# Scales of a modulation moved to TensorE, copies of rows moved to DMA queues, and low parts of the retention moved from GpSimd to VectorE

## The chip, the cores and the metric

The kernel runs on one core of a Trainium2 chip. The metric is the device time of one execution in microseconds (us); lower is better. PE is TensorE, DVE is VectorE, ACT is ScalarE, POOL is GpSimd, SP is the engine whose queue issues most DMAs (SPq in the views).

## The reference, cut to what matters

Two layers (`DEPTH = 2`) of a block with three token mixers run over 512 image tokens `x` and 256 context tokens `z`, with 1024 features. Before each mixer the tokens are scaled and shifted per feature; scale and shift come from a conditioning vector:

```
mod_x = jax.nn.silu(c) @ p['w_ada'] + p['b_ada']          # 6 x 1024 values, for x
mod_z = jax.nn.silu(c_ctx) @ p['w_ada'] + p['b_ada']      # and for z
sh1x, sc1x, g1x, sh2x, sc2x, g2x = split(mod_x, 6)
hx = x * (1.0 + sc1x) + sh1x
hz = z * (1.0 + sc1z) + sh1z
mix_x, mix_z = token_mixers(hx, hz, ...)   # hx @ w_in, then retention, neighborhood attention, MLA
x = layer_norm(ALPHA * x + g1x * mix_x)
x = layer_norm(ALPHA * x + g2x * sq_relu_mlp(x * (1.0 + sc2x) + sh2x))
```

The retention scores each chunk against itself with a decay mask in two directions, adds the product of the queries with a running state, normalises per head and gates the result. Its queries and keys are rotated first (`x1*cos - x2*sin`, `x1*sin + x2*cos`). The second layer leaves out the outputs of `z`.

## The kernel before, in words

Feature-major tiles of 128 features by 512 (or 256) tokens stay on the chip. A float32 product is done as three products in a rounded float32 form (`mm3`, L428 to L430): each operand is split into a high part, rounded by ACT (`hi_of`, L381), and a low part, the rest, by a subtraction (`lo_of`, L384) that runs on DVE unless another engine is handed in. Weights come from DRAM in units of 128 x 1024 (512 KB) through SP's queue (`fetch_in`, L390) and are split the same way.

The order on each engine is set by a scheduler that works out due times for the whole program; within it generators of work (`fill`, `pend`) are fed between the steps of the attention pipelines, so that TensorE has projections to do while the chains of an attention item run on the other engines. Every queue, SP's and POOL's among them, runs its instructions in the order that the scheduler gave it.

**The opening** (`opening`, `inputs`, L1575 to L1615). For each k of 8 feature tiles two units of `w_ada` are loaded (kind 1 is the scale, kind 0 the shift), then the tile of `x` and of `z`. `modulation` makes scale and shift from a unit by a product with the conditioning vector, summed along the row: an instruction of DVE at L496 (128 x 1024, named CUSTOM_DVE_ANT_0 in the trace). Three of the four sums of a tile are DVE's; the fourth (the shift for `z`) is a product by POOL (L492) and a sum by ACT (L493). `affine_split` then writes the scaled tile twice by ACT (L581 in full, L584 rounded) and the low part by POOL (L384, names `op<-mh,op`). TensorE multiplies the tile with four units of `w_in` (`outer`; 12 products of 512 columns and 9 of 256 per tile).

**The copies of rows.** `stacked` puts the high part of a head on 64 partitions and copies it, and the low part, to the other 64 (L665, L666, by POOL); the keys of the neighborhood attention (names `nop`, `nlo`) and the queries of the retention (`op`) go through it. L1311 does the same for the states of the retention (`st`).

**The retention** (`Retention`). `prep` makes the operands for two heads: the rotation multiplies by cosine on DVE (L1220) and by sine on POOL (L1221, `rb`) after four DMAs that swap rows (L1219, `rb<-ra`); the decayed keys are split with the low part on POOL (`t<-ktf,t`); the decay tables are multiplied by a mask on POOL (L1269). `item` has three steps: s0 scores, decay (L1349) and a split of the result with the low part on POOL (`pf<-pf,pf`), s1 products and statistics (L1373 to L1391, with a power on POOL at L1386), s2 the transposed output (L1398).

Of the kernel before, what the change touches and what calls it, by code (L numbers as in the profile page):

```python
# [16 lines left out]
DEPTH = 2  # L17
# [36 lines left out]

# [40 lines left out]
def pack_weights(inp):  # L98
# [10 lines left out]
    for l in range(DEPTH):  # L109
# [5 lines left out]
        for c in range(48):  # L115
            put(("ada", c), wa[:, 128 * c : 128 * c + 128].T)
        for n, c in (("rq", 2), ("rk", 2), ("nq", 4), ("nk", 4), ("pq", 2), ("pkv", 2), ("g0", 8), ("g1", 8), ("g2", 8)):
# [193 lines left out]
def block_kernel(ctx, tc, xT, zT, cond, wu, sp, bias, tab, out):  # L311
# [82 lines left out]


    spt = []
    for l in range(DEPTH):
# [54 lines left out]

    MOD_ADJUST = ((0, 1), (1, 1), (0, 0.5 / ALPHA), (0, 1), (1, 1), (0, 1.0 / ALPHA))

# [6 lines left out]
    def conditioning(banks):  # L461

        v = sgl("silu")
        v, h = v[:, :16], v[:, 16:32]
        fetch_in(v, cond)
        act.activation(h, v, AF.Tanh, scale=0.5)
        dve.scalar_tensor_tensor(v, h, 1.0, v, ALU.add, ALU.mult)
        cs = cond_tiles()
        for t in range(2):
            for i in range(2):  # L470
                ps = banks()
                spread(ps, 0, v[:, 8 * t + 4 * i : 8 * t + 4 * i + 4], 512)
                dst = cs[t][:, 512 * i : 512 * i + 512]
                if i:
                    dve.tensor_copy(dst, ps)
                else:
                    act.activation(dst, ps, AF.Copy)
        return cs

# [5 lines left out]

    def modulation(l, c, raw, cs, pinned=False, shared=()):

        for t in shared:  # L490
            h = dbl("prod")
            pool.tensor_tensor(h, raw, cs[t], op=ALU.mult)  # L492
            act.activation(h, h, AF.Copy, scale=0.5, accum_out=mods[l][:, c, t : t + 1])  # L493
            dve.tensor_scalar(mods[l][:, c, t : t + 1], mods[l][:, c, t : t + 1], spt[l][:, SP_BADA + c : SP_BADA + c + 1], 0.0, op0=ALU.add, op1=ALU.add)
        for t in [t for t in range(2) if t not in shared and (t == 0 or c < 16 or l < DEPTH - 1)]:
            i = dve.tensor_tensor_reduce(cs[2], raw, cs[t], 0.5, spt[l][:, SP_BADA + c : SP_BADA + c + 1], ALU.mult, ALU.add, mods[l][:, c, t : t + 1])  # L496
            if pinned:
                tc.keep_in_program_order(i)
        m = mods[l][:, c, : 2 if c < 16 or l < DEPTH - 1 else 1]
        add, mul = MOD_ADJUST[c // 8]  # L500
        if (add, mul) != (0, 1):
            dve.tensor_scalar(m, m, float(add), float(mul), op0=ALU.add, op1=ALU.mult)

# [149 lines left out]
    def stacked(dst, src, scale, view, mixed):  # L653

        xs, lows = dst
        for o, x in enumerate(xs):
            r, q = (slice(0, 64), slice(64, 128))[:: 1 - 2 * o]  # L660
            hi_of(view(x)[r], src[r], scale)
            lo = x[q] if mixed else lows[o][r]
            dve.scalar_tensor_tensor(R(view(lo)), src[r], scale, view(x)[r], ALU.mult, ALU.subtract)
            if not mixed:
                pool.tensor_copy(R(x[q]), x[r])  # L665
                pool.tensor_copy(R(lows[o][q]), lows[o][r])  # L666

# [483 lines left out]
    class Retention:  # L1151
# [39 lines left out]
        def prep(self, p2):  # L1191
# [20 lines left out]
            def rotated(name, scale, zneed, mixed):  # L1212
# [7 lines left out]
                dve.tensor_tensor(a, a, cos, op=ALU.mult)  # L1220
                pool.tensor_tensor(b, b, sin, op=ALU.mult)  # L1221
                dve.tensor_tensor(a, a, b, op=ALU.add)
# [26 lines left out]
            for src, i0 in ((k32, 0), (kz32, 4)):  # L1249
# [4 lines left out]
                for i in range(nt):  # L1254
# [5 lines left out]
                    hi_of(t[:, :256], f)  # L1260
                    lo_of(t[:, 256:], f, t[:, :256], pool)
                yield cost(512)

            gm = new_tiles(512, 2)
            for o in range(2):
                for dr in range(2):
                    c = 4 * dr + 2 * p2 + o
                    act.activation(gm[o][:, 256 * dr : 256 * dr + 256], dist[:, 256 * dr : 256 * dr + 256], AF.Exp, scale=lg[:, c : c + 1])
                pool.tensor_tensor(gm[o], gm[o], mask, op=ALU.mult)  # L1269

# [33 lines left out]
            for which in range(2):  # L1304
                for dr in range(2):
# [4 lines left out]
                    lo_of(v[own, :, 1], src, v[own, :, 0])  # L1310
                    pool.tensor_copy(R(t[other]), t[own])  # L1311

# [15 lines left out]
        def item(self, p2, o, c):  # L1328
# [4 lines left out]
            def s0():  # L1333
# [11 lines left out]
                for d, parts in ((0, ((0, 0, 256), (384, 0, 128))), (384, ((256, 256, 256), (0, 384, 128)))):  # L1345
                    f = sgl("pf")[:, :384]
                    e = 0
                    for a, b, n in parts:
                        dve.tensor_tensor(f[:, e : e + n], sc[:, a : a + n], gm[o][:, b : b + n], op=ALU.mult)  # L1349
                        e += n  # L1350
                    split_into((t[:, d : d + 384], u[:, d : d + 384]), f, pool)
                st["p"] = [(t[:, :384], u[:, :384]), (t[:, 384:], u[:, 384:])]
# [218 lines left out]
    def opening():  # L1571
# [11 lines left out]
        hx, hz = new_operand(NX, KT), new_operand(NZ, KT)  # L1583
        cs = conditioning(bank_t)
        busy(N_IDLE[1], cs[1])
        bx = [bank_d(), bank_d(), bank_t(), bank_t()]
        bz = [bank_s()[:, :256], bank_s()[:, :256], bank_d()[:, :256]]

        def inputs(k):

            for kind in (1, 0):
                raw = dbl("ada")
                fetch_in(raw, wu[IDX[0, "ada", 8 * kind + k]])
                modulation(0, 8 * kind + k, raw, cs, shared=(1,) if kind == 0 else ())
            t, u = sgl("x0"), sgl("z0")[:, :NZ]
            fetch_in(t, xT[128 * k : 128 * k + 128, :])
            fetch_in(u, zT[128 * k : 128 * k + 128, :])
            return t, u

        ws = first_weights(0, (0, 1), spare=True)  # L1600
        tiles = inputs(0)
        ws += first_weights(0, (2, 3), spare=True)
        for k in range(KT):
            ahead = inputs(k + 1) if k + 1 < KT else None
            for h, t, tok in ((hx[k], tiles[0], 0), (hz[k], tiles[1], 1)):
                affine_split(h, t, mod(0, 1, k, tok), mod(0, 0, k, tok), pool, True)
            tiles = ahead
# [257 lines left out]
```

## Time and profile before

| what | us |
|---|---|
| median of 3 runs (2626.32 to 2634.21) | 2628.12 |
| profiled execution, its own time | 2628.3 |
| its span, first to last instruction | 2626.5 |
| PE busy, share of the span | 2515.5 (96%) |
| DVE busy | 1782.5 (68%) |
| ACT busy | 1155.7 (44%) |
| POOL busy | 333.4 (13%) |
| mean granted clock of PE, share of full | 0.980 |

The span is cut in the views in stretches of time. A row of such a table gives the busy time of each engine in the stretch, the clock that TensorE was granted (1.00 is 2.4 GHz, 0.50 is 1.2 GHz, values between them a mix of the two levels) and what the DMA engines moved. In a row on waits the engine on the left stood idle until the one on the right was done.

### The profile page before, as it was taken

To read this page: it belongs to the slowest core of one execution; us is meant where nothing else is said; L and a number is where in the kernel's file an instruction comes from. 1 tells how busy PE (TensorE), PEld (TensorE's weight loads), DVE (VectorE), ACT (ScalarE), POOL (GpSimd) and SP (SyncE) were. 2 spreads that over 40 slices of the span, in tenths; PEclk is the share of its full clock that TensorE was granted. 3 is DMA by queue.
4 is the path that set the end of the run, shared out by engine and by line. 5 is a ranking of instruction groups with operands and counts; after the bars stand their busy time and mean duration, and the time that the engine had idled before them with its cause. 6 is when DMAs were issued, how large, how long until landed. Compare 5 with 4: busy or idle time off the path is not lost. (4 is left out here: it accounts for less than half of the span.)

```text
span 2626.5 us, 39849 instructions
## 1 busy us (share of the span) xinstructions
PE 2515.5 (96%) x15218; PEld 2234.2 (85%) x15218; DVE 1782.5 (68%) x3434; ACT 1155.7 (44%) x2176; POOL 333.4 (13%) x321
## 2 busy tenths in 40 slices
PE   6999999998999998999999999999999899999997
PEld 4899998987888877888888878889888788988887
DVE  8566556777878886667556767665668768744457
ACT  4555545564333345322222446554555434732325
POOL 6201102234202000000000000010214310000000
PEclk7999999999999999999999999999999999999998
DMA  6222223423565633444444424323343356433333
GB/s 241 80 82 81 70 81 110 128 79 112 200 229 169 200 120 103 125 131 137 125 132 137 136 83 138 98 82 105 109 145 99 113 192 193 137 105 96 97 97 121
DMA packets 142995, 329.43 MB, mean 125 GB/s; under 512 B 16978, under 2 KB 54738, under 8 KB 142804
## 3 DMA queue, kind: packets, MB, share of 16 engines
q1 hardware_dynamic: 132436, 311.15, 38.6%
q10 hardware_dynamic: 10368, 15.73, 1.6%
q8 instruction: 120, 1.97, 0.3%
q14 instruction: 71, 0.58, 0.1%
HBM read 288.27 MB, written 36.45 MB: 124 GB/s over the span
## 5 line engine op out<-in xcount | busy, mean ns | idle before, releaser
L428 PE MATMUL pd<-op,wsp 128*128 128x512 f32 (+1 forms) x3080 | 1074.0, 350 | 29.1 <-ACT op L584 9.6
L429 PE MATMUL pd<-op,wsp 128*128 128x512 f32 (+1 forms) x3080 | 1071.9, 348 | 6.5 <-POOL op L384 4.9
L430 PE MATMUL pd<-op,wsp 128*128 128x512 f32 (+1 forms) x3080 | 1065.3, 347 | 11.6 <-DVE wsp L384 11.6
L428 PEld LDWEIGHTS pd<-op,wsp 128*128 128x128 f32 x3080 | 588.4, 191 | 104.7 <-ACT op L584 11.5
L430 PEld LDWEIGHTS pd<-op,wsp 128*128 128x128 f32 x3080 | 588.2, 191 | 83.9 <-DVE wsp L384 13.9
L429 PEld LDWEIGHTS pd<-op,wsp 128*128 128x128 f32 x3080 | 589.9, 192 | 78.0 <-POOL op L384 8.5
L381 ACT ACTIVATE wsp<-wraw 128x1024 fp32r<-128x1024 f32 x319 | 336.4, 1055 | 425.5 <-PE pd L430 295.0
L384 DVE TENSOR_TENSOR wsp<-wraw,wsp 128x1024 fp32r<-128x1024 f32 x319 | 392.0, 1232 | 190.6 <-ACT wsp L381 189.8
L643 PE MATMUL pd<-wsp,op 128*128 128x256 f32 x704 | 201.8, 287 | 2.1 <-DVE pr L753 1.6
L645 PE MATMUL pd<-wsp,op 128*128 128x256 f32 x704 | 200.5, 285 | 0.9 <-DVE wsp L384 0.9
L644 PE MATMUL pd<-wsp,op 128*128 128x256 f32 x704 | 200.2, 285 | 0.0
L1752 DVE TENSOR_TENSOR rl<-rl 128x256 f32<-128x256 f32 (+1 forms) x104 | 58.9, 567 | 149.8 <-ACT rl L1751 149.8
L384 DVE TENSOR_TENSOR pt<-pst,pt 128x512 fp32r<-128x512 f32 (+1 forms) x208 | 121.7, 604 | 47.1 <-ACT pt L381 45.3
L1522 POOL TENSOR_TENSOR tiny<-tiny,half 128x2 f32<-128x2 f32 (+1 forms) x8 | 9.0, 1128 | 1129.1 <-DVE tiny L1521 621.9
L1751 ACT ACTIVATE rl<-pd 128x256 f32<-128x256 f32 (+1 forms) x104 | 51.7, 498 | 226.3 <-PE pd L430 226.1
L1766 DVE TENSOR_TENSOR t<-pd,t 128x512 f32<-128x512 f32 (+1 forms) x132 | 80.9, 616 | 88.3 <-PE pd L430 87.9
L643 PEld LDWEIGHTS pd<-wsp,op 128*128 128x128 f32 x704 | 136.0, 193 | 3.2 <-issue 2.4
L645 PEld LDWEIGHTS pd<-wsp,op 128*128 128x128 f32 x704 | 135.8, 193 | 1.4 <-DVE wsp L384 1.4
L644 PEld LDWEIGHTS pd<-wsp,op 128*128 128x128 f32 x704 | 135.9, 193 | 0.1
L381 ACT ACTIVATE pt<-pst 128x512 fp32r<-128x512 f32 (+1 forms) x208 | 105.1, 529 | 51.7 <-PE pst L595 39.4
L612 PE MATMUL pso<-pt,t 128*128 128x256 f32 x704 | 114.7, 292 | 7.8 <-DVE ntx L619 2.4
L496 DVE CUSTOM_DVE_ANT_0 cond<-graw,cond,sp 128x1024 bf16<-128x1024 f32 x80 | 102.4, 1280 | 18.8 <-DMA graw<-wu 18.6
(280 smaller groups left out, 3667.4 us busy)
## 6 DMA issues: line engine op xcount, KB each, us to landing
wraw<-wu SPq DMA_DIRECT2D x327, 512.0 KB, 3.7
graw<-wu SPq DMA_DIRECT2D x56, 512.0 KB, 3.7
ada<-wu SPq DMA_DIRECT2D x40, 512.0 KB, 5.5
gg<-gate ACTq DMA_DIRECT2D x48, 256.0 KB, 2.0
gl<-gg SPq DMA_DIRECT2D x48, 256.0 KB, 3.3
zbias<-bias SPq DMA_DIRECT2D x64, 128.0 KB, 2.3
t<-vd SPq DMA_DIRECT2D x28, 256.0 KB, 5.3
gd<-gt SPq DMA_DIRECT2D x40, 128.0 KB, 2.2
```

What stands on the lines that cost most here:

```text
L381: act.activation(R(dst), src, AF.Copy, scale=scale)
L384: (eng or dve).tensor_tensor(R(dst), src, hi, op=ALU.subtract)
L428: pe.matmul(ps, R(a[0]), R(b[0]), start=start, stop=False)
L429: pe.matmul(ps, R(a[0]), R(b[1]), start=False, stop=False)
L430: pe.matmul(ps, R(a[1]), R(b[0]), start=False, stop=stop)
L496: i = dve.tensor_tensor_reduce(cs[2], raw, cs[t], 0.5, spt[l][:, SP_BADA + c : SP_BADA + c + 1], ALU.mult, ALU.add, mods[l][:, c, t : t + 1])
L612: pe.matmul(o, R(vts[k]), R(pts[k]), start=k == 0, stop=k == n - 1)
L643: pe.matmul(ps, R(a[0]), R(w[0][:, o : o + 256]), start=k == 0, stop=False)
L644: pe.matmul(ps, R(a[1]), R(w[0][:, o : o + 256]), start=False, stop=False)
L645: pe.matmul(ps, R(a[0]), R(w[1][:, o : o + 256]), start=False, stop=k == nk - 1)
L1752: dve.tensor_tensor(t, t, t, op=ALU.mult)
L1766: dve.tensor_tensor(a, ps, a, op=ALU.add)
```

## The change

Five edits. (1) In the opening the scale (kind 1) is computed on TensorE: a float32 product of the unit, now packed with features of the input on the partitions, with the two conditioning vectors (8 products of 2 columns per tile), and one DVE instruction that reads the result; DVE computes both sums of the shift; POOL's product and ACT's sum are gone. `+1` is folded into the bias once, so the small instructions at L502 go for the scales. (2) `affine_split` in the opening uses DVE for the full tile and for the low part. (3) The first tile's inputs are loaded ahead of the first weights, and the conditioning vector ahead of everything. (4) The copies of rows in `stacked` and of the states are DMAs on SP's queue. (5) The retention's low parts (`t<-ktf`, `pf`) and the sine product are DVE's, and the mask is applied to two of the four 128-column blocks of a table.

```
+ADA_PE = [(0, c) for c in range(8, 16)]
...
-            put(("ada", c), wa[:, 128 * c : 128 * c + 128].T)
+            w = wa[:, 128 * c : 128 * c + 128]
+            put(("ada", c), fm(w) if (l, c) in ADA_PE else w.T)
...
+    def modulation_pe(ps, l, c, raw, v):
+        for k in range(KT):
+            pe.matmul(ps, raw[:, 128 * k : 128 * k + 128], v[:, :, k], start=k == 0, stop=k == KT - 1)
+        m = mods[l][:, c, :]
+        dve.tensor_scalar(m, ps, 0.5, spt[l][:, SP_BADA + c : SP_BADA + c + 1], op0=ALU.mult, op1=ALU.add)
+        adjust(m, c)
...
-        for t in shared:
-            h = dbl("prod")
-            pool.tensor_tensor(h, raw, cs[t], op=ALU.mult)
-            act.activation(h, h, AF.Copy, scale=0.5, accum_out=mods[l][:, c, t : t + 1])
...
-                pool.tensor_copy(R(x[q]), x[r])
-                pool.tensor_copy(R(lows[o][q]), lows[o][r])
+                sync.dma_start(x[q], x[r])
+                sync.dma_start(lows[o][q], lows[o][r])
...
-                pool.tensor_tensor(b, b, sin, op=ALU.mult)
+                dve.tensor_tensor(b, b, sin, op=ALU.mult)
...
-                    lo_of(t[:, 256:], f, t[:, :256], pool)
+                    lo_of(t[:, 256:], f, t[:, :256])
...
-                pool.tensor_tensor(gm[o], gm[o], mask, op=ALU.mult)
+                ends, cut_off = (t.rearrange("p (e n) -> p e n", n=128)[:, 0:4:3] for t in (gm[o], mask))
+                pool.tensor_tensor(ends, ends, cut_off, op=ALU.mult)
...
-                    pool.tensor_copy(R(t[other]), t[own])
+                    sync.dma_start(t[other], t[own])
...
-                    split_into((t[:, d : d + 384], u[:, d : d + 384]), f, pool)
+                    split_into((t[:, d : d + 384], u[:, d : d + 384]), f)
...
-                modulation(0, 8 * kind + k, raw, cs, shared=(1,) if kind == 0 else ())
+                if kind:
+                    modulation_pe(bank_o()[:, :2], 0, 8 * kind + k, raw, v)
+                else:
+                    modulation(0, k, raw, cs)
...
-                affine_split(h, t, mod(0, 1, k, tok), mod(0, 0, k, tok), pool, True)
+                affine_split(h, t, mod(0, 1, k, tok), mod(0, 0, k, tok), dve)
```

What follows are places in the order of the instructions. First DVE in the opening, in the kernel before, for one tile and the start of the next; ada_214 is the unit of a scale, ada_219 of a shift, and the rows without an input read out a sum.

```order
L496 ISA cond_138,mod_103<-ada_214,cond_138,sp_93 128x1024
L496 ISA mod_103 128x1
L496 ISA cond_138,mod_103<-ada_214,cond_139,sp_93 128x1024
L496 ISA mod_103 128x1
L502 TENSOR_SCALAR mod_103<-mod_103 128x2
L496 ISA cond_138,mod_103<-ada_219,cond_138,sp_93 128x1024
L496 ISA mod_103 128x1
L494 TENSOR_SCALAR mod_103<-mod_103,sp_93 128x1
```

The same place in the changed kernel: pso_300 is the bank into which TensorE wrote the scale of the tile after the next, x_55 and z_56 are the tiles to be split, ada_310 is the unit of a shift.

```order
L494 TENSOR_SCALAR mod_105<-pso_300,sp_95 128x2
L596 TENSOR_SCALAR mh_318<-x_55_265,mod_105 128x512
L596 TENSOR_SCALAR mh_322<-z_56_266,mod_105 128x256
L389 TENSOR_TENSOR op_128<-mh_318,op_128 128x512
L512 ISA cond_141,mod_105<-ada_310,cond_141,sp_95 128x1024
L512 ISA mod_105 128x1
L389 TENSOR_TENSOR op_135<-mh_322,op_135 128x256
L512 ISA cond_141,mod_105<-ada_310,cond_142,sp_95 128x1024
L512 ISA mod_105 128x1
```

Two of the four large sums remain on DVE, and the two tiles and their low parts come to it. TensorE in the opening, in the kernel before, at the end of one tile and the start of the next (op_123 and op_130 are the tiles of `x` and `z`, op_124 the next of `x`):

```order
L429 MATMUL pss_174<-op_130,wsp_183 128x256
L430 MATMUL pss_174<-op_130,wsp_183 128x256
L429 MATMUL pd_175<-op_130,w_204 128x256
L430 MATMUL pd_175<-op_130,w_205 128x256
L428 MATMUL pd_169<-op_124,wsp_178 128x512
L428 MATMUL pd_170<-op_124,wsp_183 128x512
```

The same place in the changed kernel (op_134 is the tile of `z`, op_128 the next of `x`, ada_298 the unit of a scale):

```order
L436 MATMUL pss_177<-op_134,wsp_206 128x256
L437 MATMUL pss_177<-op_134,wsp_206 128x256
L436 MATMUL pd_178<-op_134,w_211 128x256
L492 MATMUL pso_300<-v_cond,ada_298 128x2 x8
L437 MATMUL pd_178<-op_134,w_212 128x256
L435 MATMUL pd_172<-op_128,wsp_201 128x512
L435 MATMUL pd_173<-op_128,wsp_206 128x512
```

The eight products of a scale stand one place ahead of the end of a tile. POOL in the first pass of the retention of layer 0, in the kernel before (t_727x are low parts of decayed keys, op copies of queries, pf low parts of an item):

```order
L384 TENSOR_TENSOR t_7274<-ktf_7299,t_7274 128x256
L384 TENSOR_TENSOR t_7274<-ktf_7303,t_7274 128x256
L1269 TENSOR_TENSOR t_7307<-t_7307,dist_6996 128x512 x2
L665 CAST op_7394<-op_7394 64x256 x2
L666 CAST op_7395<-op_7395 64x256
L1221 TENSOR_TENSOR rb_7373<-rb_7373,rot_6993 128x512
L666 CAST op_7395<-op_7395 64x256
L665 CAST op_7382<-op_7382 64x512 x2
L666 CAST op_7383<-op_7383 64x512
L384 TENSOR_TENSOR pf_7415<-pf_7416,pf_7414 128x384
L666 CAST op_7383<-op_7383 64x512
L384 TENSOR_TENSOR pf_7415<-pf_7421,pf_7414 128x384
```

POOL at the same place in the changed kernel, in full (rs are powers of the statistics, nyz a sum of the attention before):

```order
L640 TENSOR_TENSOR nyz_6720<-tz_6966,fo_6970 64x256
L1401 TENSOR_TENSOR rs_7160<-rs_7160,half 128x4
L1401 TENSOR_TENSOR rs_7290<-rs_7290,half 128x4
L1284 TENSOR_TENSOR t_7342<-t_7342,dist_7031 128x2x128 x2
L1401 TENSOR_TENSOR rs_7482<-rs_7482,half 128x4
```

Of the twelve rows one pair is left, half as wide. SP's queue in the neighborhood attention of layer 0, in the kernel before (zbias is the bias of one item, wraw a weight):

```order
L888 DMA my_3_256_850<-my_4215 128x256
L1035 DMA zbias_4029<-bias 128x256 x3
L390 DMA wraw_5403<-wu 128x1024
L1035 DMA zbias_4029<-bias 128x256 x2
L390 DMA wraw_5706<-wu 128x1024
```

The same place in the changed kernel:

```order
L901 DMA my_3_256_885<-my_4250 128x256
L1048 DMA zbias_4064<-bias 128x256 x2
L678 DMA nop_4695<-nop_4695 64x512
L679 DMA nlo_4696<-nlo_4696 64x512
L678 DMA nop_4695<-nop_4695 64x512
L679 DMA nlo_4696<-nlo_4696 64x512
L678 DMA nop_4705<-nop_4705 64x256
L679 DMA nlo_4706<-nlo_4706 64x256
L678 DMA nop_4705<-nop_4705 64x256
L1048 DMA zbias_4064<-bias 128x256
L395 DMA wraw_5438<-wu 128x1024
L679 DMA nlo_4706<-nlo_4706 64x256
```

Eight copies of a pair of heads now stand between the loads of biases and weights.

## Rows read from the trace of the kernel before

**Rows 1.** Page, part 1: busy us of TensorE and GpSimd, instructions.

```profile
PE 2515.5 (96%) x15218; PEld 2234.2 (85%) x15218; DVE 1782.5 (68%) x3434; ACT 1155.7 (44%) x2176; POOL 333.4 (13%) x321
```

**Rows 2.** Stretches of 50 us: length, busy us per engine, granted clock, DMA, GB/s.

```profile
0.00:50.00 50.00, 33.51 (x100) 22.43 (x101) 43.05 (x51) 22.20 (x35) 28.98 (x18) 0.79 0.81 286
50.00:100.00 50.00, 42.93 (x254) 36.53 (x254) 36.82 (x63) 29.85 (x56) 24.71 (x15) 0.90 0.23 75
...
650.00:700.00 50.00, 39.09 (x241) 35.28 (x240) 40.41 (x115) 18.67 (x39) 20.23 (x22) 0.93 0.34 115
...
800.00:850.00 50.00, 48.76 (x308) 43.68 (x307) 44.41 (x128) 16.82 (x33) 15.33 (x12) 1.00 0.58 174
...
2000.00:2050.00 50.00, 44.43 (x289) 40.49 (x288) 38.78 (x88) 23.73 (x53) 24.56 (x24) 0.90 0.37 105
```

**Rows 3.** Waits of TensorE in 0 to 100 us: total, times, longest.

```profile
PE pd L428 <- ACT op L584: 8.6, 5, 4.1
PE pd L429 <- POOL op L384: 4.9, 6, 2.5
PE pss L428 <- ACT op L584: 4.8, 3, 2.5
```

**Rows 4.** Timeline of the opening, VectorE: start, duration, what.

```profile
40.71 3.50 DVE L496 CUSTOM_DVE_ANT_0 cond<-ada,cond,sp 128x1024 bf16<-128x1024 f32 x1
...
44.14 0.20 DVE L494 TENSOR_SCALAR mod<-mod,sp 128x1 f32<-128x1 f32 x1
44.27 1.27 DVE L496 CUSTOM_DVE_ANT_0 cond<-ada,cond,sp 128x1024 bf16<-128x1024 f32 x1
...
59.39 1.27 DVE L496 CUSTOM_DVE_ANT_0 cond<-ada,cond,sp 128x1024 bf16<-128x1024 f32 x1
```

**Rows 5.** The same timeline, GpSimd.

```profile
40.73 2.40 POOL L492 TENSOR_TENSOR prod<-ada,cond 128x1024 f32<-128x1024 f32 x1
```

**Rows 6.** Timeline of TensorE: products at the lower and higher clock, sums in float32.

```profile
25.66 0.63 PE L429 MATMUL pst<-op,w 128*128 128x512 f32 x1
...
26.08 0.63 PE L430 MATMUL pst<-op,w 128*128 128x512 f32 x1
...
55.99 0.39 PE L429 MATMUL pst<-op,w 128*128 128x512 f32 x1
56.22 0.39 PE L430 MATMUL pst<-op,w 128*128 128x512 f32 x1
...
78.94 1.84 PE L720 MATMUL pso<-ones,sq 128*128 128x1 f32 x16
```

**Rows 7.** VectorE, 500 to 710 us, by shape: busy us, mean ns, idle before.

```profile
L606 DVE TENSOR_SCALAR p<-p,tiny 128x512 f32<-128x512 f32 x16 | 8.8, 549 | 0.3
...
L384 DVE TENSOR_TENSOR t<-pd,t 128x256 fp32r<-128x256 f32 x14 | 5.8, 414 | 0.3 <-ACT t L381 0.2
...
L1222 DVE TENSOR_TENSOR ra<-ra,rb 128x512 f32<-128x512 f32 x4 | 2.8, 688 | 2.8 <-POOL rb L1221 2.7
```

**Rows 8.** Stretches of 5 us in the opening, columns as in Rows 2.

```profile
10.00:15.00 5.00, 5.00 (x13) 2.30 (x11) 4.78 (x5) 0.34 (x1) 3.26 (x1) 1.00 1.05 401
```

**Rows 9.** Waits of TensorE in 500 to 720 us.

```profile
PE pst L1373 <- DVE ro L1377: 6.5, 1, 6.5
...
PE pd L1253 <- DVE ra L1222: 2.3, 1, 2.3
```

**Rows 10.** Timeline of GpSimd inside the wait of 6.5 us.

```profile
646.26 2.72 POOL L1269 TENSOR_TENSOR t<-t,dist 128x512 f32<-128x512 f32 x2
...
656.50 0.99 POOL L384 TENSOR_TENSOR pf<-pf,pf 128x384 fp32r<-128x384 f32 x1
```

**Rows 11.** Waits of TensorE in 1950 to 2120 us.

```profile
PE pd L1253 <- DVE ra L1222: 3.7, 1, 3.7
```

**Rows 12.** GpSimd by shape, whole span: busy us, mean ns, idle before.

```profile
L384 POOL TENSOR_TENSOR pf<-pf,pf 128x384 fp32r<-128x384 f32 x40 | 47.8, 1211 | 181.9 <-ACT pf L381 160.4 <-issue 21.2
```

**Rows 13.** Page, part 6: DMA issues, KB each, median us to landing.

```profile
rb<-ra SPq DMA_DIRECT2D x32, 64.0 KB, 2.0
```

More of the change, by code (lines that the diff above doesn't have):

```diff
@@ L393, in fetch_in @@
             tc.keep_in_program_order(i)
+    v_cond = const.tile([128, 2, KT], F32, name="v_cond")
+    fetch_in(v_cond, cond.rearrange("p (t k) -> p t k", t=2))
     spt = []
@@ L451, in block_kernel @@
     mods = [const.tile([128, 48, 2], F32, name=f"mod{l}") for l in range(DEPTH)]
-    MOD_ADJUST = ((0, 1), (1, 1), (0, 0.5 / ALPHA), (0, 1), (1, 1), (0, 1.0 / ALPHA))
+    MOD_ADJUST = (1, 1, 0.5 / ALPHA, 1, 1, 1.0 / ALPHA)
+    for t in spt:
+        b = t[:, SP_BADA : SP_BADA + 48].rearrange("p (h k c) -> p h k c", h=2, k=3)[:, :, 1]
+        dve.tensor_scalar(b, b, 1.0, 0.0, op0=ALU.add, op1=ALU.add)
     silu = [dram.tile([1, D], F32, name=f"silu{i}") for i in range(2)]
@@ L461, in conditioning @@
     def conditioning(banks):
-        v = sgl("silu")
-        v, h = v[:, :16], v[:, 16:32]
-        fetch_in(v, cond)
+        v = v_cond
+        h = sgl("silu")[:, :16].rearrange("p (t k) -> p t k", t=2)
         act.activation(h, v, AF.Tanh, scale=0.5)
@@ L471, in conditioning @@
                 ps = banks()
-                spread(ps, 0, v[:, 8 * t + 4 * i : 8 * t + 4 * i + 4], 512)
+                spread(ps, 0, v[:, t, 4 * i : 4 * i + 4], 512)
                 dst = cs[t][:, 512 * i : 512 * i + 512]
@@ L477, in conditioning, with adjust @@
                     act.activation(dst, ps, AF.Copy)
-        return cs
+        return v, cs
+    def modulation_pe(ps, l, c, raw, v):
[4 more added lines that the diff above has]
+        adjust(m, c)
+    def adjust(m, c):
+        mul = MOD_ADJUST[c // 8]
+        if mul != 1:
+            dve.tensor_scalar(m, m, 0.0, float(mul), op0=ALU.add, op1=ALU.mult)
     def conditioning_again():
@@ L484, in conditioning_again, with modulation @@
         return cs
-    def modulation(l, c, raw, cs, pinned=False, shared=()):
-        for t in shared:
-            h = dbl("prod")
-            pool.tensor_tensor(h, raw, cs[t], op=ALU.mult)
-            act.activation(h, h, AF.Copy, scale=0.5, accum_out=mods[l][:, c, t : t + 1])
-            dve.tensor_scalar(mods[l][:, c, t : t + 1], mods[l][:, c, t : t + 1], spt[l][:, SP_BADA + c : SP_BADA + c + 1], 0.0, op0=ALU.add, op1=ALU.add)
-        for t in [t for t in range(2) if t not in shared and (t == 0 or c < 16 or l < DEPTH - 1)]:
+    def modulation(l, c, raw, cs, pinned=False):
+        nt = 2 if c < 16 or l < DEPTH - 1 else 1
+        for t in range(nt):
             i = dve.tensor_tensor_reduce(cs[2], raw, cs[t], 0.5, spt[l][:, SP_BADA + c : SP_BADA + c + 1], ALU.mult, ALU.add, mods[l][:, c, t : t + 1])
@@ L498, in modulation @@
                 tc.keep_in_program_order(i)
[L499 to L502, printed above, removed]
+        adjust(mods[l][:, c, :nt], c)
     class Paced:
@@ L1583, in opening @@
         hx, hz = new_operand(NX, KT), new_operand(NZ, KT)
-        cs = conditioning(bank_t)
-        busy(N_IDLE[1], cs[1])
+        v, cs = conditioning(bank_t)
+        busy(N_IDLE[1], idle)
         bx = [bank_d(), bank_d(), bank_t(), bank_t()]
@@ L1598, in inputs @@
             return t, u
+        tiles = inputs(0)
         ws = first_weights(0, (0, 1), spare=True)
-        tiles = inputs(0)
         ws += first_weights(0, (2, 3), spare=True)
```

## The prediction

> **What bounds the kernel now.** I read the page first: TensorE is busy for 2515.5 of 2626.5 us [rows 1], so 111 us of idle time, and what a low clock costs beside it, are all that an edit off TensorE can win. The table of stretches says where it lies [rows 2]. In 0 to 100 us TensorE is idle for 16.5 + 7.1 = 23.6 us at a clock of 0.79 and 0.90, with VectorE busy for 43 of the first 50 us and GpSimd for 29; in 650 to 700 us it is idle for 10.9 us, in 2000 to 2050 for 5.6, again at a lowered clock and with GpSimd busy for 20 to 25 us. GpSimd's share of the whole span is 13%, but it sits where TensorE waits. I then asked for TensorE's waits there [rows 3, 9, 11], and for the timeline of the engines that they name [rows 4, 5, 10].
>
> **The opening, before.** The waits are for tiles from ScalarE and low parts from GpSimd [rows 3]; behind both stand VectorE's large sums. One sum takes 1.27 us alone, but 3.50 us where GpSimd's product of 2.40 us (start 40.73) lies beside it [rows 4, 5]. The sums that start at 44.27 and at 59.39 stand at the same place two tiles apart, so a tile takes 15.1 / 2 = 7.56 us [rows 4]. The float32 sums that follow the last tile start at 78.94 [rows 6]; I take that as the end of the opening.
>
> **The opening, after.** GpSimd has nothing to do in it, so I take VectorE's large sums at 1.27 us. On VectorE a tile then has: the scale read from TensorE's bank, 0.20 (as the short instruction in rows 4); the two full tiles, 0.55 [rows 7] and about 0.3 (half of it); the low part of `x`, 0.69; a large sum with its read-out, about 1.35; the low part of `z`, 0.41 [rows 7]; and one more large sum, 1.35. That is 4.85 us of work. On TensorE a product of 512 columns starts every 0.23 us at full clock and every 0.42 at the lower one [rows 6]; with half for 256 columns a tile's 12 + 9 products take 12 x 0.23 + 9 x 0.12 = 3.8 us, or 6.9 at the lower clock. New are 8 float32 products of 2 columns. The nearest row is 8 products of one column with the same kind of weights: 16 instructions in 1.84 us [rows 6]. So 5.6 us per tile on TensorE.
>
> Neither is the cycle, because the order ties them: the scale of the tile after next stands behind nearly all products of the current tile, and VectorE's first instruction waits for it. From a low part of `z` at T: five products of 256 columns 0.6, the scale 1.84, two hand-overs of about 0.1 (estimated), then VectorE 0.20 + 0.55 + 0.3 + 0.69 + 1.35 + 0.41, which gives T + 6.1 us. VectorE's second sum (1.35) lies beside the scale on TensorE. So 6.1 us per tile against 7.56.
>
> The start: the loads ahead of the second tile are about 4.5 MB; at the 401 GB/s of the queue when nothing holds it [rows 8], from about 5 us on, they land by 16 us. The scale of the second tile then runs at the lower clock, as TensorE stood idle before it (3.7 us, to 20), and VectorE's chain of 0.20 + 0.55 + 0.3 + 0.69 + 1.35 + 0.41 puts the first low part of `z` at about 24 us. Six cycles and one of 3.3 without a scale make 24 + 36.6 + 3.3 = 64; the last products end about 2 us later, and some 4 us are lost at the lower clock until TensorE has been dense for a while, as at 25.66 us in the run before [rows 6]. The end of the opening comes to 70 us instead of 79: **9 us won**. Bounds: 13 (full clock from the start) and -24 (each cycle at the lower clock: 0.6 and 1.84 doubled and 12 x 0.42 of the next tile behind VectorE's low part make 10 us, and an end at 103 us). I take the upper side, since a TensorE that is busy for 5.6 of 6.1 us leaves only short gaps, and dense stretches in the run before ran at 0.23 [rows 6]. ScalarE loses two full tiles and a sum per tile; it isn't late there, so that counts nothing.
>
> **The retention.** One wait stands out, 6.5 us at L1373 [rows 9]. GpSimd works without a gap from 646.26, with the mask (2.72), copies of queries, the sine product and at last the low part of the item that TensorE needs (656.50) [rows 10]. In the change only half a mask is left there, and the low part comes from VectorE. I count 5 of the 6.5 us. The waits for the rotation (2.3 in layer 0, 3.7 in layer 1 [rows 9, 11]) have the sine product of GpSimd in their chain; VectorE's takes 0.69 instead, so 1 us each. Half a microsecond each for the short waits on GpSimd's low parts in the two layers, and 1 to 2 us of clock that comes back behind the long wait: -5 - 2 - 1 - 1.5 = **-9.5 us**.
>
> Against this VectorE gets work: 40 low parts of 384 columns (between 0.41 for 256 and 0.69 for 512, so 0.55), 24 of 256 at 0.41, 8 products at 0.69: 22 + 10 + 5.5 = 37 us over four passes [rows 7, 12]. It is busy for 40.4 of 50 us in 650 to 700 and 44.4 in 800 to 850 [rows 2], so there is room for it in each stretch (a quarter of 37 is 9 us, over passes of 50 to 100 us), but the chains of an item have VectorE on them three times. GpSimd's low part took 1.21 us [rows 12], so the chain itself gets shorter by 0.65 per low part; queueing takes part of it back. I count **+4 us** for all passes, between 0 and +22 (every low part of an item late by its own length).
>
> By the Trainium skill (SBUF — State Buffer, section "SBUF: two separate sides") an instruction of VectorE with two inputs in the on-chip memory and one of GpSimd that reads it lock each other out in full. The sum of 3.50 us beside a product of 2.40 agrees: 1.27 + 2.40 = 3.67. By that rule the moved instructions free more of VectorE's time than they take, and the +4 would be 0 or below.
>
> **The copies.** 104 copies (64 keys, 24 queries, 16 states, counted in the code) leave GpSimd for SP's queue. A transfer of 64 KB between rows lands in 2.0 us [rows 13]; these are 64 and 128 KB, so 2 to 2.5. All are made a pair of heads or a pass ahead, behind products of 5 us and more, so their latency is covered; if that is gone, each group costs 2.5 us. What stands behind them on SP's queue are the bias of the next item and a weight: if a copy waits there for its low part, the bias comes late, VectorE waits, and the item with it. Eight groups in the neighborhood attention; from 0 to 2 us each, I take 0.1: **+1 us**.
>
> **Sum.** -9 - 9.5 + 4 + 1 = -13.5 against the profiled execution of 2628.3 us, which is the median of the runs within 0.2 us. I say 2615 us.
>
> **The rivals.**
> - *More of it:* the opening without the low clock (-13) and the idle time of 10.9 and 5.6 us in the two stretches [rows 2] gone with it, with VectorE's time free as above: 2628 - 13 - 15 = 2600. For it: GpSimd stands in each of these stretches. Against: VectorE and the statistics are in the same chains.
> - *SP's queue becomes the wait:* 8 groups x 1 us, so 2622. For it: copies stand between the loads of biases. Against: both loads are asked for an item ahead.
> - *TensorE's float32 sums cost twice the row:* 3.7 us per scale, the cycle is then 7.9 us, the opening ends at 80, and nothing is won there: 2625. The row of 1.84 us speaks against it. The Trainium skill (FP8 and Floating Point Precision, "TensorE Precision Notes") gives four passes for a true float32 product; the row has two instructions for each.
> - *VectorE becomes the bound of the passes:* place, the items of the retention; price, 40 low parts x 0.55 = 22 us instead of 4, and the 6.5 us wait stays as one on VectorE: 2628 - 9 - 3 + 22 + 1 = 2639. It decides once VectorE's order holds an item's low part behind work of the next pass; 44.4 of 50 us busy [rows 2] speaks for it, the room in the other stretches against.
>
> **How the numbers follow.** The forecast (2606 to 2624) has 0.62, more of it 0.13, SP's queue 0.10, dear float32 sums 0.05, VectorE 0.10. Runs of this kernel tell 0.3% apart, or 8 us: faster is below 2620, slower above 2636. Of the forecast 0.53 lie below 2620; with 0.13 and 0.04 of SP's queue that makes 0.70 for faster; 0.09 + 0.06 + 0.05 = 0.20 for the same; 0.10 slower. From 2598 to 2634 all but the last rival and the edges are held.
>
> **What would show it.** In the profile after: large sums of 1.27 us throughout, a step of about 6 us per tile and float32 sums that start near 70 us; 16 instructions per scale in under 2 us; no wait of TensorE over 3 us in the retention's first pass; no wait of VectorE for a bias. I am wrong if the opening's end stays near 79, if TensorE's idle time in 600 to 700 us doesn't shrink, or if waits for VectorE's low parts take its place.

## The result, and the profile after

The changed kernel takes 2612.99 us (median of 4 runs, 2612.38 to 2615.55) against 2627.74 before: 14.8 us less, ratio 0.9943 with a 95% interval of 0.993 to 0.9955. 2615 was forecast. Its profiled execution took 2613.25 us, with a span of 2611.4 at a mean granted clock of 0.983. The total is as forecast; the terms that made it are not, as the experiments show.

The page of the changed kernel, part 1 (busy us, share, instructions) [rows 1]:

```profile
PE 2523.3 (97%) x15346; PEld 2246.8 (86%) x15346; DVE 1771.6 (68%) x3492; ACT 1140.0 (44%) x2144; POOL 135.6 (5%) x121
```

The same stretches as in [rows 2], and one more behind the fourth (length, busy us of PE, PEld, DVE, ACT, POOL, then granted clock, DMA share, GB/s):

```profile
0.00:50.00 50.00, 42.42 (x220) 34.11 (x221) 30.30 (x60) 13.78 (x18) 0.20 (x4) 0.90 0.88 316
50.00:100.00 50.00, 48.28 (x292) 44.21 (x291) 27.40 (x68) 22.40 (x44) 6.13 (x5) 0.86 0.16 54
...
650.00:700.00 50.00, 44.28 (x257) 38.99 (x258) 46.71 (x122) 16.57 (x35) 3.86 (x3) 0.97 0.61 207
800.00:850.00 50.00, 48.62 (x301) 43.29 (x301) 46.63 (x135) 13.17 (x25) 4.15 (x4) 1.00 0.49 148
850.00:900.00 50.00, 44.81 (x274) 39.00 (x272) 42.01 (x78) 17.13 (x28) 0.00 (x0) 1.00 0.64 206
2000.00:2050.00 50.00, 44.00 (x306) 40.72 (x304) 42.27 (x116) 24.63 (x53) 4.62 (x5) 0.93 0.37 102
```

TensorE's idle time in the first 100 us fell from 23.6 to 9.3 us and in 650 to 700 from 10.9 to 5.7, but the clock in 50 to 100 us is lower than before (0.86 against 0.90), and 850 to 900 us now has 5.2 us of idle time.

VectorE in the opening (start, duration), as [rows 4], and TensorE's sums, as [rows 6]:

```profile
29.02 0.22 DVE L494 TENSOR_SCALAR mod<-pso,sp 128x2 f32<-128x2 f32 x1 [2.54 <-PE pso L492]
30.53 1.28 DVE L512 CUSTOM_DVE_ANT_0 cond<-ada,cond,sp 128x1024 bf16<-128x1024 f32 x1
...
35.11 0.22 DVE L494 TENSOR_SCALAR mod<-pso,sp 128x2 f32<-128x2 f32 x1 [1.75 <-PE pso L492]
```

```profile
33.23 1.84 PE L492 MATMUL pso<-v_cond,ada 128*128 128x2 f32 x16
...
67.86 2.00 PE L733 MATMUL pso<-ones,sq 128*128 128x1 f32 x16
```

A tile takes 35.11 - 29.02 = 6.09 us, a sum 1.28, a scale 1.84, and the float32 sums start at 67.86 instead of 78.94. Behind them, in stretches of 10 us:

```profile
60.00:70.00 10.00, 9.65 (x57) 8.13 (x55) 5.58 (x13) 5.40 (x13) 0.00 (x0) 1.00 0.00 0
70.00:80.00 10.00, 9.80 (x58) 9.81 (x58) 2.39 (x6) 4.68 (x10) 1.72 (x2) 0.66 0.09 29
80.00:90.00 10.00, 9.01 (x52) 8.43 (x51) 8.44 (x18) 5.26 (x10) 3.13 (x2) 0.66 0.49 157
```

The clock falls from 1.00 to 0.66, in two stretches: it is 0.51 from 70.2 to 77.1 us and from 80.4 to 87.3 us, and 1.00 in the 3.3 us between them. TensorE's waits in 500 to 720 us, as [rows 9] (total, times, longest):

```profile
PE pd L1303 <- DVE t L389: 3.5, 2, 2.4
PE pd L1266 <- DVE ra L1235: 1.9, 1, 1.9
PE pss L684 <- DVE pf L1364: 1.9, 2, 0.9
```

The wait of 6.5 us at the items' products is gone; waits for VectorE's low parts of the keys (3.5) are new.

How far the changed kernel is ahead, from the starts of the same instructions in both traces (such a place is called a landmark below):

| landmark | before | after | ahead |
|---|---|---|---|
| first float32 sums behind the opening | 78.9 | 67.9 | 11.0 |
| first transpose of a maximum (L595, L608) | 135.3 | 130.3 | 5.0 |
| first transposed output of the retention | 642.6 | 629.1 | 13.5 |
| last one of layer 0's first pass | 702.3 | 687.7 | 14.6 |
| last one of its second pass | 862.4 | 846.9 | 15.5 |
| first sums of squares of a layer norm | 936.5 | 926.7 | 9.8 |
| last transposed output of layer 1 | 2169.1 | 2159.3 | 9.8 |
| first sums of squares of layer 1's first norm | 2224.4 | 2211.5 | 12.9 |
| end of the span | 2626.5 | 2611.4 | 15.1 |

So 6 us of the opening's 11 are given back at once, 5.7 us of the retention's gain in the branches behind its second pass, and 5.3 us come in at the end, where the change has no line. The first loss is the lower clock's. Between the first two landmarks TensorE has the same 410 instructions and nearly the same idle time (1.6 and 1.8 us), but is busy for 5.8 us longer; first the kernel before, then the changed one:

```profile
78.90:135.30 56.40, 54.85 (x410) 51.61 (x409) 34.89 (x75) 32.63 (x70) 8.69 (x7) 1.00 0.35 106
67.90:130.30 62.40, 60.61 (x410) 57.37 (x410) 34.78 (x75) 33.60 (x71) 8.70 (x7) 0.89 0.31 96
```

At the end two stretches of 30 us ran at 0.94 of the clock in the kernel before (2160 to 2190 and 2250 to 2280); the same work in the changed kernel ran at 1.00. That is 1.8 us each, the rest is idle time. With one profiled execution of each kernel it isn't shown that the change raised this clock: e7 below, which differs from the changed kernel in one edit, had 0.94 and 0.89 there.

### The profile page after: what moved, and what is told of

The parts are those of the page before. It is cut to its first block, busy times and chain, and to the rows that moved or that the text cites. A ratio compares the mean times of both kernels' runs of the same rounds, so it can differ in the third digit from the quotient of the medians.

```text
span 2611.4 us, 40080 instructions
## 1 busy us (share of the span) xinstructions
PE 2523.3 (97%) x15346; PEld 2246.8 (86%) x15346; DVE 1771.6 (68%) x3492; ACT 1140.0 (44%) x2144; POOL 135.6 (5%) x121
## 4 chain that ended last, share of the span: by engine, by line
PE 79%; DVE 10%; issue 3%; ACT 3%; DMA 2%; POOL 1%; SPq 1%; POOLq 0%; DVEq 0%; ACTq 0%
PE pd L437 20%; PE pd L436 20%; PE pd L435 20%; PE pso L625 3%; PE pst L608 3%; PE pd L658 3%; PE pd L656 3%; PE pd L657 3%; DVE op L389 1%; PE pss L436 1%; PE pss L435 1%; PE pss L437 1%; DVE wsp L389 1%; PE pss L684 1%; ACT wsp L386 1%
## 5 line engine op out<-in xcount | busy, mean ns | idle before, releaser
L1445 ACT ACTIVATE gate<-pd 128x512 f32<-128x512 f32 x72 | 37.9, 527 | 165.1 <-PE pd L437 156.8
```

## The experiments

All are timed in five rounds, each beside the kernel before on the same chip. O, C and R are the opening's, the copies' and the retention's edits; negative is faster. The medians of the kernel before that they are set against lie between 2627.16 and 2629.07 us, so a difference between two rows can change by 2 us with the way it is taken; below, a difference from the changed kernel is that of the medians in the first column.

| kernel | us (median) | against before | ratio, 95% interval |
|---|---|---|---|
| e1: O | 2623.04 | -5.8 | 0.9977 (0.9967 to 0.9987) |
| e2: R | 2634.49 | +5.7 | 1.0022 (1.0013 to 1.0031) |
| e3: C | 2621.90 | -6.9 | 0.9976 (0.9967 to 0.9985) |
| e4: all, scores' low parts on GpSimd in second passes | 2612.44 | -16.4 | 0.9935 (0.9922 to 0.9949) |
| e5: O, C | 2613.36 | -15.7 | 0.9943 (0.9931 to 0.9956) |
| e6: R, C | 2619.27 | -9.8 | 0.9966 (0.9954 to 0.9979) |
| e7: all, scores' low parts on GpSimd | 2609.50 | -19.6 | 0.9926 (0.9913 to 0.9938) |
| e8: all, 12 sums between products | 2612.71 | -16.4 | 0.9942 (0.9928 to 0.9955) |
| e9: as e7, 20 sums between products | 2610.80 | -16.4 | 0.9935 (0.9922 to 0.9947) |
| e10: all, scales made twice | 2634.61 | +7.5 | 1.0025 (1.0014 to 1.0035) |
| e11: all, GpSimd's product put back | 2627.78 | +0.6 | 1.0001 (0.9992 to 1.0010) |
| e12: as e7, keys' low parts on GpSimd too | 2609.94 | -17.2 | 0.9934 (0.9922 to 0.9947) |

**The parts alone.** e1 is before with the edits (1) to (3), e2 with (5), e3 with (4), each as the diff above shows it.

> The kernel before with the opening's edits alone. Theory from the landmarks of the changed kernel: the float32 sums behind the opening start 11 us earlier, but the clock falls while they run, and the first maximum's transposes at 130 us are only 5 us earlier; so the span is 5 us shorter than before (3 to 8), and the sums' stretch runs at 1.2 GHz. Rival, the prediction's term: the end of the opening is what the kernel gains, so 9 to 11 us shorter and no lowered clock behind 70 us.

The landmarks held: sums at 68.1 us, first transpose of a maximum at 130.7, and -5.8 us in the end. The clock in 70 to 90 us is 0.66 here too.

> The kernel before with the retention's edits alone (low parts of the keys and of the weighted scores and the sine products by VectorE, half a mask on GpSimd; copies stay on GpSimd). Theory from the landmarks: 7 us won in layer 0's first pass, 1 in its second, about 6 given back in the branches by waits for VectorE, 3 to 5 won in layer 1, so 5 to 9 us shorter than before; the 6.5 us wait gone. Rival, the prediction's sum for this part: -9.5 + 4, so 5.5 shorter. Rival, VectorE as the bound: 10 us longer.

R alone is slower: the theory and the first rival missed in sign, VectorE as the bound has the sign and about half of its size. The wait of 6.5 us is gone here too, and R is 7.1 us ahead at the first transposed output (635.5 against 642.6), but only 0.5 ahead at the last of the pass: from 635 to 702 us TensorE now waits 3.6 us instead of 2.1 for VectorE to weight scores, 2.9 instead of 1.6 for it to read an output's bank, and 2.6 instead of nothing for a gate from ScalarE. GpSimd and VectorE in this stretch (start, duration):

```profile
648.37 2.15 POOL L665 CAST op<-op 64x512 fp32r<-64x512 f32 x2 [2.84 <-ACT op L381]
650.08 1.74 DVE L384 TENSOR_TENSOR pf<-pf,pf 128x384 fp32r<-128x384 f32 x2
650.58 1.71 POOL L666 CAST op<-op 64x512 fp32r<-64x512 f32 x2
...
657.20 0.55 DVE L384 TENSOR_TENSOR pf<-pf,pf 128x384 fp32r<-128x384 f32 x1
```

Two low parts take 1.74 us where GpSimd's copies lie beside them, and 0.55 each where none does: the copies that stay on GpSimd now stretch what was moved to VectorE. That is 0.6 us of the 6.6 lost in this pass; the rest isn't shown by these rows.

> The kernel before with the 104 copies as transfers on SP's queue alone. Theory and prediction: hidden, within 2 us of before. Rival: the copies of queries and states leave GpSimd in 646 to 656 us, so the low part behind them starts earlier and the 6.5 us wait shrinks by half, 3 us shorter. Other rival: SP's queue holds the bias, 8 us longer.

Both the first and the queue's rival missed: C alone wins 6.9 us. The rival on the copies of queries and states has the sign and less than half of the size. The wait of 6.5 us in e3:

```profile
PE pst L1373 <- DVE ro L1377: 4.1, 1, 4.1
PE pd L1253 <- DVE ra L1222: 3.2, 1, 3.2
```

In the kernel before, GpSimd's timeline between the two rows of [rows 10]:

```profile
649.05 1.28 POOL L665 CAST op<-op 64x256 fp32r<-64x256 f32 x2
650.39 0.40 POOL L666 CAST op<-op 64x256 fp32r<-64x256 f32 x1
650.87 1.29 POOL L1221 TENSOR_TENSOR rb<-rb,rot 128x512 f32<-128x512 f32 x1
652.22 0.92 POOL L666 CAST op<-op 64x256 fp32r<-64x256 f32 x1
653.61 2.15 POOL L665 CAST op<-op 64x512 fp32r<-64x512 f32 x2 [0.47 <-ACT op L381]
655.82 0.61 POOL L666 CAST op<-op 64x512 fp32r<-64x512 f32 x1
```

Five of the six are copies, 5.4 of 6.7 us, and the low part of the item stands behind them. Yet only 2.4 of the 6.5 us went with them. In e3 GpSimd has nothing to do ahead of this low part and waits for the rounded scores from ScalarE, which come from VectorE:

```profile
653.00 1.95 POOL L384 TENSOR_TENSOR pf<-pf,pf 128x384 fp32r<-128x384 f32 x2 [4.47 <-ACT pf L381]
```

So what is left of the wait, 4.1 us, lies in the chain ahead of the low part and not in GpSimd's queue. By the landmarks e3 is 5.2 us ahead at the last output of this pass and 7.3 at the end; how the gain divides beyond the 2.4 us isn't shown.

**In company.** e5 has O and C, e6 has R and C.

> The kernel before with the opening's edits and the copies as transfers; the retention's low parts, sine products and whole mask stay on GpSimd. Theory A (the single edits measured add up: -6 for the opening, -6.5 for the copies; the retention's edits, +5.7 alone, turn to a gain only where GpSimd's copies are gone): 12 to 13 us shorter than before, 2616, and 2 to 4 us longer than the changed kernel. Rival B (the retention's edits are a loss in every company): 15 to 19 shorter than before, so faster than the changed kernel by 2 or more.

> The kernel before with the retention's edits and the copies, the opening as before. Theory A (VectorE's new low parts cost because GpSimd's copies of 0.6 to 1.0 us lie beside them and stretch them; without the copies that is gone): 8 to 10 us shorter than before, so more than the sum of the two alone (+5.7 - 6.5 = -0.8). Rival (the edits add up, the rest of the changed kernel's gain comes from the opening): within 2 us of before.

e6's time is that of theory A: R costs 5.7 us beside GpSimd's copies and nothing without them. The 2.9 us that it seems to win there (-6.9 to -9.8) are not clear of the noise, as the intervals of e3 and e6 overlap. That the copies change R's price is shown (by 8.6 us in the medians); theory A's reason, the stretching, covers little of it. Over the whole span the 40 low parts of the scores take 1.4 us longer in e2 than in e6 (busy us, mean ns; e2 first):

```profile
L384 DVE TENSOR_TENSOR pf<-pf,pf 128x384 fp32r<-128x384 f32 x40 | 23.5, 610 | 0.5
L384 DVE TENSOR_TENSOR pf<-pf,pf 128x384 fp32r<-128x384 f32 x40 | 22.1, 574 | 0.5
```

Where the rest comes from stays open. e5 fits neither fully: with O and C in place R is worth nothing (2613.36 to 2612.99, both 0.9943 of before).

**What of R is worth something.** e4, e7 and e12 give low parts back to GpSimd:

```
-                    split_into((t[:, d : d + 384], u[:, d : d + 384]), f)
+                    split_into((t[:, d : d + 384], u[:, d : d + 384]), f, pool)              # e7, e12
+                    split_into((t[:, d : d + 384], u[:, d : d + 384]), f, pool if p2 else dve)   # e4
...
-                    lo_of(t[:, 256:], f, t[:, :256])
+                    lo_of(t[:, 256:], f, t[:, :256], pool)                                   # e12
```

> The changed kernel with the low parts of the weighted scores by VectorE in the first pass alone; in the second, where VectorE is busy for 44 of 50 us, they go back to GpSimd. Theory (VectorE's load costs what is lost in the second pass and the branches behind it): 3 to 6 us shorter than the changed kernel, about 2608. Rival (what is lost in the branches doesn't come from these low parts): the same as the changed kernel within 2 us, or longer, as GpSimd's low part takes 1.2 us in each item's chain.

> The changed kernel with the low parts of the weighted scores on GpSimd in both passes; the keys' low parts, the sine products and the half mask stay as changed. Theory (the 6.5 us wait went because GpSimd's queue is empty, not because VectorE makes the low part): within 3 us of the changed kernel. Rival, the prediction's step (VectorE's low part saves 0.65 us in each item's chain and the wait): 5 to 8 us longer than the changed kernel.

> The changed kernel with both kinds of the retention's low parts on GpSimd (weighted scores and keys); the sine products stay on VectorE and the half mask on GpSimd. Theory (what is left to win over the opening and the copies alone, 2613.4, is GpSimd's queue ahead of the first items: mask and sine product; the keys' low parts are moved at no gain): 2608 to 2611, as with the score's low parts alone on GpSimd. Rival (the keys' low parts on VectorE are what wins 4 us): 2613 to 2614.

e7's rival is out: with the scores' low parts on GpSimd the kernel is not slower but 3.5 us faster than the changed kernel (4.8 when each is set against its own runs of the kernel before). The wait of 6.5 us does not come back; the waits that answer to [rows 9] in e7:

```profile
PE pss L684 <- DVE pf L1364: 2.9, 2, 2.4
PE pd L1266 <- DVE ra L1235: 2.1, 1, 2.1
...
PE pst L1388 <- POOL pf L389: 0.7, 2, 0.4
```

By the landmarks e7 is ahead of the changed kernel by 2.7 us at the last output of layer 0's first pass (685.0), by 5.5 at the first layer norm (921.2), by 8.4 at the last output of layer 1's first pass (2057.1 against 2065.5), by 9.6 at the last output of layer 1 (2149.7) and by 3.6 at the end of the span. So the lead grows in more than one place, and 6 us of it are missing at the end, where e7's profiled execution had the low clock named above. One of the places is the stretch from the last output of layer 0's second pass to the first layer norm. In the kernel before, the changed kernel and e7:

```profile
862.40:936.50 74.10, 70.72 (x451) 63.80 (x449) 62.63 (x115) 26.17 (x41) 0.00 (x0) 1.00 0.65 200
```

```profile
846.90:926.70 79.80, 74.47 (x457) 66.27 (x456) 66.25 (x118) 26.05 (x42) 0.00 (x0) 0.98 0.61 192
```

```profile
845.90:921.20 75.30, 71.86 (x451) 64.92 (x449) 62.48 (x111) 26.06 (x41) 0.00 (x0) 0.98 0.64 198
```

The changed kernel has 2.6 us of TensorE's and 3.8 us of VectorE's work left over there against e7, and 1.9 us more of idle time. R alone (78.0 us in this stretch) and R with C (79.9) show it, O with C (75.0) doesn't. TensorE's other work is ordered anew in each kernel, so a landmark also moves with the work that stands ahead of it (457 instructions against 451 here). Moving the keys' low parts back as well (e12) changes nothing in the time, as its theory had it, though 2.3 us of the wait at the items' products come back. e4's theory missed and its rival holds: it is no faster than the changed kernel by more than the runs can tell. Its last output of layer 1 starts at 2159.1 us, as in the changed kernel (2159.3), which points to the low parts of the first passes, which e4 leaves on VectorE, for what e7 wins up to there. The intervals of e4, e7, e9 and e12 overlap each other's and that of the changed kernel; e7's lies lowest, and it has the shortest median of the study. It is the best version found, and its lead over the changed kernel rests on medians and the trace, not on separate intervals.

**The opening's price.** e10 makes each scale twice, e11 puts GpSimd's product back:

```
+        for n in range(2):
             for k in range(KT):
                 pe.matmul(ps, raw[:, 128 * k : 128 * k + 128], v[:, :, k], start=k == 0, stop=k == KT - 1)
...
                     modulation(0, k, raw, cs)
+                    pool.tensor_tensor(dbl("prod"), raw, cs[1], op=ALU.mult)
```

> The changed kernel with each scale's 8 float32 products made twice over (the result is the same). Theory (the scale lies on the chain that makes the cycle, 6.1 us, and costs its row): a tile takes 1.84 us more, 7.9, the sums behind the opening start at 80 instead of 68 us, and the time grows by 6 to 13 us. Rival (TensorE's scale lies beside VectorE's second sum and is hidden): the cycle stays at 6.1 and the time within 2 us of the changed kernel.

The cost is 21.6 us over the changed kernel, more than the theory's 13, and the sums behind the opening start at 94.5 us. e10 in TensorE's timeline and the clock:

```profile
31.56 4.21 PE L493 MATMUL pso<-v_cond,ada 128*128 128x2 f32 x32
41.90 4.30 PE L493 MATMUL pso<-v_cond,ada 128*128 128x2 f32 x32
52.58 4.70 PE L493 MATMUL pso<-v_cond,ada 128*128 128x2 f32 x32
```

```profile
30.00:60.00 30.00, 30.00 (x155) 27.44 (x154) 11.38 (x23) 2.87 (x5) 0.00 (x0) 0.67 0.39 134
```

```profile
30.00:60.00 30.00, 29.18 (x186) 25.59 (x185) 21.33 (x45) 7.08 (x10) 0.00 (x0) 1.00 0.54 182
```

The second row of 30 to 60 us is the changed kernel's. A tile takes 10.3 to 10.7 us: the stretch has a granted clock of 0.67, a mix of 1.2 and 2.4 GHz, although TensorE never stands idle. The tile comes close to the 10 us of the forecast's lower bound, but by other terms: twice the scales at 0.67, where the bound has one scale throughout at the lower clock. In the changed kernel itself the bound was not met.

> The changed kernel with GpSimd's product of the opening put back (weights times a row of the conditioning, 128x1024), whose result nobody reads. Theory (GpSimd's product and VectorE's sums keep each other out, 3.50 us for a sum beside it before): one sum per tile takes 3.4 to 3.7 us again, a tile 7 to 8 us, the sums start at 74 to 80 us, and 3 to 9 us are lost. Rival (the gain of the opening comes from the work taken off VectorE, not from GpSimd's silence): sums stay at 1.27, the time within 2 us of the changed kernel.

GpSimd's product alone costs 14.8 us, all that the change won and beyond the theory's 3 to 9. VectorE and GpSimd in e11:

```profile
26.23 3.38 DVE L512 CUSTOM_DVE_ANT_0 cond<-ada,cond,sp 128x1024 bf16<-128x1024 f32 x1
...
29.24 2.60 POOL L1613 TENSOR_TENSOR prod<-ada,cond 128x1024 f32<-128x1024 f32 x1 [0.71 <-DMA ada<-wu]
...
29.54 2.57 DVE L389 TENSOR_TENSOR op<-mh,op 128x256 fp32r<-128x256 f32 x1
```

A low part that takes 0.42 us alone takes 2.57 beside it. The theory's place was half right: here it is a low part or a tile that is hit as often as a sum. The opening's end moved by 21 us, to 88.9, more than seven locked instructions: the clock was 0.50 in 20 to 30 and in 50 to 60 us, and TensorE waited 3.1 us for a unit of weights to land. How the 21 us divide between the three stays open.

**The clock behind the opening.** e8 and e9 lay the one-column sums between the products that stand beside them anyway (24 products of 256 columns, kept in this order):

```
-            kx_.sums()
-            kz_.sums()
...
+            for i in range(nt):
+                for j, q in enumerate(nd.sq):
+                    pe.matmul(ss[:, i : i + 1], q[:, 128 * i : 128 * i + 128], ones, start=j == 0, stop=j == 1)
+                    some(2)        # e8: two products after each of 12 sums; e9: one after each of 20
```

> The changed kernel with the opening's first 12 float32 sums of one column laid between the 24 products of 256 columns that stand beside them, two products after each sum; the same work. Theory (the clock fell to 1.2 GHz at 70 us because TensorE had run nothing but one-column sums and waited for a square): the clock stays at 2.4 GHz behind 70 us, and 4 to 6 us come back, about 2608. Rival (the clock falls in any case, or at the next 16 sums at 78 us): the same as the changed kernel within 2 us.

> The changed kernel with the low parts of the weighted scores on GpSimd, and with the first 20 float32 sums behind the opening laid one by one between the 24 products of 256 columns. Theory (the clock falls when only one-column sums run for some 2 us and a wait stands beside them, and two thirds of the sums now have a product beside them): the low clock behind the opening gets shorter than the 17 us of the changed kernel, 2 to 4 us come back, and with the 3.5 us of the low parts the time is 2605 to 2608. Rival (the clock's fall costs nothing that isn't made up later): as the kernel with the low parts on GpSimd alone, 2609.5 within 1.5 us.

Both theories fell, and both rivals hold in time: e8 is 0.3 us from the changed kernel and e9 1.3 us from e7. 70 to 80 and 80 to 90 us in e8, then in e9:

```profile
70.00:80.00 10.00, 9.40 (x66) 8.75 (x66) 5.56 (x12) 6.59 (x14) 2.74 (x3) 0.81 0.25 79
80.00:90.00 10.00, 9.87 (x57) 9.70 (x58) 6.22 (x15) 4.46 (x7) 2.50 (x2) 0.67 0.41 121
```

```profile
70.00:80.00 10.00, 9.97 (x58) 9.62 (x57) 3.96 (x9) 5.58 (x12) 1.72 (x2) 0.64 0.11 29
80.00:90.00 10.00, 10.00 (x49) 10.00 (x50) 5.74 (x12) 3.90 (x7) 3.54 (x2) 0.51 0.50 157
```

In e8 the mixed sums still ran at full clock; the fall shows at the sums that were left over (8 sums, two instructions each), in TensorE's timeline:

```profile
73.71 0.48 PE L1653 MATMUL pss<-op,w 128*128 128x256 f32 x2
...
75.15 2.38 PE L733 MATMUL pso<-ones,sq 128*128 128x1 f32 x16
...
77.75 0.41 PE L657 MATMUL pd<-wsp,op 128*128 128x256 f32 x1
```

In e9 it fell earlier and deeper, with TensorE busy for 9.97 and 10.00 of each 10 us. What makes it fall stays open.

## Why the prediction came out right, and which steps were wrong

- **The opening's cycle: right.** 6.09 us against 6.1, the scale 1.84, large sums 1.28, the first low part of `z` at 24.85 against 24, the sums at 67.9 against 70.
- **"I take that as the end of the opening: 9 us won": wrong.** e1 gives 6. The place where I stopped counting lies ahead of a stretch that ran at full clock before and at 0.66 after; 11 us became 5 by 130 us. No term stood for a clock that changes level behind the edit; that clock is nearly the whole of the loss (5.8 us of longer busy time for the same 410 instructions).
- **The low end of that term (each cycle at the lower clock): not met.** From 30 to 60 us the changed kernel ran at 1.00. e10 shows that the clock can fall in the cycles themselves, at twice the scales.
- **The retention's -9.5: the failed step.** I counted 5 of the 6.5 us of the wait as time won, for the emptier queue and the low part from VectorE. The wait does go, and in R alone too, but R alone is 5.7 us slower: in the same pass TensorE waits longer for VectorE and ScalarE instead. Nor is it the scores' low part that takes the wait away: C alone takes 2.4 us off, and e7, where this low part is GpSimd's still, has none of it. R's measured worth is +5.7 alone, -2.9 beside C (not clear of the noise), nothing beside O and C.
- **VectorE's load, +4: near in size for the scores' low parts, and in other places too.** e7 gives 3.5 by medians. By the landmarks it lies in the first passes of both layers and in the branches behind layer 0's second pass, which the term did not have. The keys' low parts add nothing (e12).
- **The rule on SBUF: right on the lock, wrong as an argument for the move.** By the Trainium skill (SBUF — State Buffer, section "SBUF: two separate sides") a VectorE instruction with two inputs in SBUF and a GpSimd instruction that reads SBUF keep each other out for a whole instruction. 1.74 us for two low parts and 2.57 for a short one agree. By that rule the +4 would have been 0 or below; the sum kept +4, and e7 speaks for the sum: the kernel is faster with the scores' low parts on GpSimd.
- **The copies, +1: wrong, -6.9.** I counted only SP's side of the move. That side was right (VectorE waits 1.3 us in all for a bias); the gain is GpSimd's time, of which 2.4 us show as a shorter wait in e3 and the rest is not divided.
- **The sum.** -9 - 9.5 + 4 + 1 = -13.5 met -14.8 by luck: the copies won 7.9 us more than their term, and the opening (-6) and the retention (nothing beside O and C) fell short by 3 and 5.5. That makes -12.9; the last 1.9 us belong to no single edit. Measured, O is worth -6 alone and -6.3 on top of R and C; C and R together -9.8.
- **The rivals.** SP's queue: out (e3). Float32 sums at twice the row: out (1.84). "More of it" needed a full clock in the opening: out. VectorE as the bound: true of R alone (e2), by 5.7 us and not by 11.

## What to carry to other kernels

When several edits empty one engine's queue, list what stands in the queue ahead of the late instruction, and then look at what else that instruction waits for: the copies were 5.4 of 6.7 us of GpSimd's queue, and taking them away shortened the wait by 2.4 of 6.5 us. A wait that goes is not yet time won; it can come back a few us later on the engine that took the work. What a move between GpSimd and VectorE costs depends on what remains on the other engine: measure the parts alone and in pairs, since R went from +5.7 to nothing, or -2.9 at best, by its company. And take the price of an edit at a landmark well behind the place, where the clock has settled, not at the first event behind it.

## What the hardware showed that I had not expected

- With twice the two-column products the clock was 0.67 instead of 1.00 over 30 us with TensorE never idle (e10): 1.84 us of work on the chain per tile cost 3.1 (21.6 over seven tiles).
- The clock can fall behind a dense opening: two stretches of 6.9 us at 0.51 with 3.3 us at 1.00 between them (products of 256 columns 0.21 us apart in the two, 0.12 before, between and after). Laying products between the one-column sums did not prevent it (e8, e9).
- Two low parts beside GpSimd's copies took 1.6 times as long (1.74 against 2 x 0.55), so a copy by GpSimd is not free even where nobody waits for it.
